# All gates leave PSUM as tanh of half their input: Silu and Sigmoid taken out of a hybrid encoder layer's later stages

## The chip, the cores and the metric

The kernel runs on one core of a Trainium2 chip. The metric is device time in microseconds (us), the median of several executions. Before the change it is 1966.65 us, over three runs from 1964.79 to 1967.43 us. The engines are called as in the profile: PE is the matrix engine (PEld is its weight load), DVE the vector engine, ACT the scalar engine that evaluates activation functions, POOL the GpSimd engine, and SP the queue from which the program issues its DMAs.

## The reference: one encoder layer with two attention branches

Two groups of 1024 tokens with 1024 channels go through the same layer. The input is normalised and modulated to `h`, and one projection `h @ w_in` gives queries, keys and values of two branches, two gate paths `za` and `zb` (512 columns each) and two merge gates `ga` and `gb` (1024 columns each):

```python
oa = gqa_attention(qa, ka, va) * jax.nn.silu(za)
ob = diff_attention(qb, kb, vb, lam)
ob = rms_norm(ob, subln_g) * (1.0 - lam_init)
ob = ob.reshape(B, S, BR_B) * jax.nn.silu(zb)
pa = jnp.einsum('bse,ed->bsd', oa, w_proj_a)
pb = jnp.einsum('bse,ed->bsd', ob, w_proj_b)
merged = jax.nn.sigmoid(ga) * pa + jax.nn.sigmoid(gb) * pb
out = jnp.einsum('bsd,de->bse', merged, w_out)
return x + gate[:, None, :] * out
```

Branch A is grouped-query attention with 8 heads; its softmax denominators are divided out late, when the gate is applied. Branch B is differential attention with 4 heads of two softmax maps each. With `silu(z) = z * sigmoid(z)` and `sigmoid(z) = (tanh(z/2) + 1) / 2`, both gate functions can be written with tanh.

## The kernel before, in words

Large products are made in two-part float32r form: each operand is split into a high and a low part, and three matmuls stand for one. The two token groups (`g` 0 and 1) run one after the other, each in these stages. The **head** makes keys, values and the first queries of branch A. **Phases 0 to 4** run attention units (score matmuls at lines 709 and 710, row maximum on DVE at line 711, exponential on ACT at line 712, a transpose on DVE at line 753, value matmuls at 768 and 785) while the input projections for later heads are made beside them. The **gated stretch** runs the last head of attention beside `gated_gen`, which multiplies attention outputs by their gates, and beside the start of the merge. Then come **merge** (`merge_gen`, line 915) and **output projection** (`out_gen`, line 944), which are almost all matmul.

The gate projections are made by `z_gen`, in twelve items per group, each of four PSUM banks of 128 x 512 (24 matmuls per bank, line 679). They are cut into small steps and woven into all stages up to the gated stretch, where they keep PE fed. Items 0 to 3 (16 banks per group) are `za` and `zb`; items 4 to 11 are `ga` and `gb`. Each bank is copied by ACT to an SBUF tile `ev` (line 685; the pool holds one such tile) and stored to DRAM by a DMA (line 688). Of the items, five banks' worth of steps lie in the head of group 0 and four in that of group 1.

In `gated_gen` the attention output `o` and the gate `z` come back by DMA (lines 867 and 868), ACT applies Silu to `z` (line 870), DVE multiplies `o` by `z` (line 875 in branch A, 881 in branch B, there with the column `subg`) and by the softmax or norm factor (line 885), and the product is split for the projection: its high part on ACT (line 886), its low part on DVE (line 887). In `merge_gen` two gate tiles at a time come back (line 905), ACT applies Sigmoid to both (line 906), and DVE multiplies the projected branch in PSUM by the gate (line 926 for branch A, 921 for branch B).

The order of instructions on each engine is set when the kernel is built: the generators are woven by tables of weights at the top of the file, attention steps have priority, and the tile framework's scheduler then places each instruction by its own model of durations. Each engine runs its list strictly in that order; SP too issues its DMAs in list order, and each waits there for its data. PSUM banks rotate: the pool `f` has three, `s` two of double width, `a` one.

## Time and profile before

| what | value |
| --- | --- |
| median of three runs | 1966.65 us (1964.79 to 1967.43) |
| the profiled execution's own time | 1970.28 us |
| its span, first to last instruction | 1968.4 us |
| busy, PE / DVE / ACT / POOL | 1900.2 / 1110.0 / 861.2 / 723.6 us |
| mean granted TensorE clock | 0.983 |

The profile is of one execution, which was 3.6 us slower than the median. An activation function outside the set that ACT holds needs an `ACT_TABLE_LOAD` before it, which the profile lists as an instruction of the line that needs it. In rows of the timeline the columns are start in us, duration in us, engine, line, operation, output `<-` inputs, shapes and count; a bracket at the end gives the idle time of the engine before it and what ended that. In rows of grouped instructions a bar separates busy time and mean duration from the idle time before them. `zd` are the gates stored in DRAM, `row` and `q` the SBUF tiles of the gated stretch, `p` the tiles of 128 x 1024 that hold exponentials and also merge gates, `st` weights as they are loaded.

### The profile page before, as it was taken

What the parts mean: (1) busy time and instruction counts of PE and PEld (TensorE: products, weight loads), DVE (VectorE), ACT (ScalarE), POOL (GpSimd) and SP (SyncE); (2) the same over time, 40 slices, a digit from 0 to 9 for tenths busy, and PEclk for the clock granted to TensorE, in tenths of its full rate; (3) what the DMA queues carried; (4) which work ended last, traced back from release to release, by engine and by line L of the source; (5) the groups of instructions that cost most, each with busy time, mean ns of one, the idle gap of its engine ahead of it and who ended that gap; (6) DMA issues with size and microseconds to landing.
All of it is one profiled execution on the core that took longest, in us unless ns stands there. A gap on an engine that the chain in (4) does not pass through costs nothing.

```text
span 1968.4 us, 29657 instructions
## 1 busy us (share of the span) xinstructions
PE 1900.2 (97%) x10466; PEld 1574.4 (80%) x10466; DVE 1110.0 (56%) x1570; ACT 861.2 (44%) x1653; POOL 723.6 (37%) x1008
## 2 busy tenths in 40 slices
PE   8899999999999998899999999999999999999999
PEld 3788778888888984778889788888888798877887
DVE  5557762444667466647464667444447735665641
ACT  4434442444445344754323445333445524567410
POOL 2463431433465251221236544124456616412110
PEclk9899999999999999999999999999999999999999
DMA  8125674546243335875641567655524423567531
GB/s 313 47 73 159 186 204 135 161 123 201 79 136 111 100 86 173 248 236 192 206 157 41 141 190 194 176 161 147 159 78 137 114 74 92 169 204 270 168 102 54
DMA packets 269011, 295.03 MB, mean 150 GB/s; under 512 B 35264, under 2 KB 217664, under 8 KB 268864
## 3 DMA queue, kind: packets, MB, share of 16 engines
q1 hardware_dynamic: 268864, 293.15, 49.9%
q8 instruction: 83, 1.36, 0.3%
q14 instruction: 64, 0.52, 0.1%
HBM read 133.59 MB, written 42.01 MB: 89 GB/s over the span
## 4 chain that ended last, share of the span: by engine, by line
PE 81%; DMA 6%; ACT 3%; POOL 3%; DVE 3%; issue 2%; SPq 2%; ACTq 0%; POOLq 0%; DVEq 0%
PE f L679 21%; PE f L496 19%; PE f L915 6%; PE a L768 6%; PE f L944 5%; PE s L709 5%; PE s L710 5%; PE s L944 4%; PE a L785 4%; PE s L915 2%; DMA row<-zd 1%; SPq L762 1%; DMA st<-in_w_in_dram 1%; PE f L547 1%; DMA q<-p 1%
## 5 line engine op out<-in xcount | busy, mean ns | idle before, releaser
L679 PE MATMUL f<-u,w 128*128 128x512 f32 x2232 | 579.3, 398 | 1.7 <-ACT w L178 1.2
L496 PE MATMUL f<-w,u 128*128 128x256 f32 x3456 | 483.6, 286 | 2.5 <-ACT ev L685 1.6
L679 PEld LDWEIGHTS f<-u,w 128*128 128x128 f32 x2232 | 411.4, 190 | 85.3 <-issue 2.7
L496 PEld LDWEIGHTS f<-w,u 128*128 128x128 f32 x3456 | 456.3, 192 | 24.1 <-issue 2.3
L711 DVE TENSOR_REDUCE m<-s 128x1 f32<-128x1024 f32 x256 | 310.2, 1219 | 240.6 <-PE s L710 238.5
L712 ACT ACTIVATE p<-s,m 128x1024 f32<-128x1024 f32 x256 | 285.1, 1114 | 241.3 <-DVE m L711 208.8
L180 POOL TENSOR_TENSOR w<-st,w 128x512 fp32r<-128x512 f32 x168 | 220.9, 1332 | 456.4 <-ACT w L178 410.9
L753 DVE STREAM_TRANSPOSE p<-p 128x1024 f32<-128x1024 f32 x192 | 237.3, 1240 | 70.3 <-ACT p L712 61.7
L514 POOL TENSOR_TENSOR rs<-ss,nhalf 128x4 f32<-128x4 f32 (+1 forms) x112 | 110.0, 982 | 329.9 <-DVE ss L513 275.2
L710 PE MATMUL s<-u,sw 128*128 128x512 f32 x512 | 206.2, 403 | 0.0
L178 ACT ACTIVATE w<-st 128x512 fp32r<-128x512 f32 x196 | 114.6, 626 | 136.0 <-DMA st<-in_w_in_dram 79.7
L915 PE MATMUL f<-u,w 128*128 128x512 f32 x552 | 134.6, 398 | 4.4 <-ACT ev L685 3.7
L785 PE MATMUL a<-q,u 128*128 128x256 f32 x512 | 130.2, 393 | 7.3 <-DMA q<-p 5.5
L915 PEld LDWEIGHTS f<-u,w 128*128 128x128 f32 x552 | 104.7, 192 | 26.8 <-ACT ev L685 3.9
L709 PE MATMUL s<-u 128*128 128x512 f32 x256 | 111.2, 434 | 12.2 <-ACT p L712 12.0
L550 DVE TENSOR_TENSOR u<-f,u 64x256 fp32r<-64x256 f32 (+1 forms) x196 | 80.4, 411 | 71.3 <-ACT u L549 66.4
L768 PE MATMUL a<-q,u 128*64 128x256 f32 x1024 | 117.7, 382 | 0.8 <-DMA q<-p 0.8
L785 PEld LDWEIGHTS a<-q,u 128*128 128x128 f32 x512 | 99.0, 198 | 23.8 <-issue 7.8
L710 PEld LDWEIGHTS s<-u,sw 128*128 128x128 f32 x512 | 98.3, 192 | 17.4 <-issue 0.8
L709 PE MATMUL s<-u,u 128*128 128x512 f32 x256 | 104.7, 410 | 4.3 <-ACT p L712 3.4
L944 PE MATMUL f<-u,w 128*128 128x512 f32 x456 | 105.6, 389 | 0.0
L508 ACT ACTIVATE row<-f 128x256 f32<-128x256 f32 (+1 forms) x112 | 41.1, 367 | 146.1 <-PE f L496 135.5
(169 smaller groups left out, 2140.9 us busy)
## 6 DMA issues: line engine op xcount, KB each, us to landing
q<-p SPq DMA_DIRECT2D x768, 128.0 KB, 2.6
st<-in_w_in_dram SPq DMA_DIRECT2D x132, 256.0 KB, 3.1
zd<-ev SPq DMA_DIRECT2D x96, 256.0 KB, 2.5
sw<-u SPq DMA_DIRECT2D x256, 64.0 KB, 2.0
p<-zd SPq DMA_DIRECT2D x64, 256.0 KB, 3.8
u<-in_w_ada_dram SPq DMA_DIRECT2D x8, 1024.0 KB, 10.4
od<-oo SPq DMA_DIRECT2D x64, 128.0 KB, 2.4
st<-in_w_in_dram SPq DMA_DIRECT2D x64, 128.0 KB, 2.7
```

Source lines behind the costliest of these rows:

```text
L180: e.tensor_tensor(out=wl, in0=st, in1=wh.bitcast(F32), op=ALU.subtract)
L496: nc.tensor.matmul(ps, lt[c][:, sl], w[:, c, wi, :], start=(k == 0), stop=(k == 23))
L679: nc.tensor.matmul(ps, w[:, c, wi, e * P : (e + 1) * P], rt[c], start=(k == 0), stop=(k == 23),)
L709: nc.tensor.matmul(s[:, sl], q, k[:, sl], start=True, stop=False)
L710: nc.tensor.matmul(s[:, sl], sw, k[:, sl], start=False, stop=True)
L711: nc.vector.tensor_reduce(out=m, in_=s, axis=AX.X, op=ALU.max, negate=True)
L712: nc.scalar.activation(pt.rearrange("p (j c a) -> p j c a", j=4, c=8), s.rearrange("p (c a j) -> p j c a", c=8, j=4), AF.Exp, bias=m, accu ...
L753: nc.vector.transpose(pt, pt)
L768: lambda k=k, m=m: nc.tensor.matmul(acc[(LO, HI)[m]], u["v"][:, k], pT[m][:, k], start=(k == 0), stop=(k == 7))
L785: nc.tensor.matmul(acc, u["v"][:, k], pT[:, k], start=(k == 0), stop=(k == 7))
L915: nc.tensor.matmul(ps, w[:, c, wi, d * P : (d + 1) * P], o[:, oi, :], start=(k == 0), stop=(k == 11))
L944: nc.tensor.matmul(ps, w[:, c, wi, e * P : (e + 1) * P], m[:, mi, :], start=(k == 0), stop=(k == 23))
```

## The change

`z_gen` now leaves PSUM by `tanh(z/2)` for every item. For `za` and `zb` a second instruction, on DVE, makes `(tanh + 1) * z` in the same tile, reading the PSUM bank once more; that is twice Silu. `gated_gen` no longer applies Silu, and `merge_gen` no longer applies Sigmoid: its multiply by the gate becomes `(tanh + 1) * projected`, one instruction as before. The halves are folded into `subg` (branch B), into the reciprocal softmax sums as they leave PSUM (branch A), and into the output gate column `gatec`.

```diff
@@ load_tables_B, gate_gen
-        nc.vector.tensor_scalar(out=subg, in0=subg, scalar1=(1.0 - LAM_INIT) * math.sqrt(2 * HD), scalar2=None, op0=ALU.mult)
+        nc.vector.tensor_scalar(out=subg, in0=subg, scalar1=0.5 * (1.0 - LAM_INIT) * math.sqrt(2 * HD), scalar2=None, op0=ALU.mult)
...
+            nc.vector.tensor_scalar(out=gatec[:, cs], in0=gatec[:, cs], scalar1=0.5, scalar2=None, op0=ALU.mult)
@@ z_gen
                 ev = mtile("ev", [P, 512], bufs=1)
-                nc.scalar.activation(ev, ps, fn)
+                nc.scalar.activation(ev, ps, AF.Tanh, scale=0.5)
+                if silu:
+                    nc.vector.scalar_tensor_tensor(out=ev, in0=ev, scalar=1.0, in1=ps, op0=ALU.add, op1=ALU.mult)
@@ gated_gen
-            nc.scalar.activation(row, ps, AF.Copy)
+            nc.scalar.activation(row, ps, AF.Copy, scale=0.5)
...
-            if i >= SILU:
-                nc.scalar.activation(z, z, AF.Silu)
@@ merge_gen
-                        nc.scalar.activation(gg, gg, AF.Sigmoid)
...
-                        nc.vector.tensor_tensor(out=g, in0=ps, in1=g, op=ALU.mult)
+                        nc.vector.scalar_tensor_tensor(out=g, in0=g, scalar=1.0, in1=ps, op0=ALU.add, op1=ALU.mult)
...
-                        nc.vector.tensor_tensor(out=md[:, d], in0=ps, in1=g, op=ALU.mult)
+                        nc.vector.scalar_tensor_tensor(
+                            out=md[:, d], in0=g, scalar=1.0, in1=ps, op0=ALU.add, op1=ALU.mult
+                        )
@@ z_item: za and zb pass silu=True, ga and gb do not
```

Line numbers shift by one or two in the changed kernel: the copy out of PSUM is line 684 there and the new DVE instruction 686, the row maximum is 712, the exponential 713, the multiply by the gate 874, the next multiply 884, the split 885 and 886. In the whole program the list of ACT has 43 table loads before and 2 after (one for the first Silu at the start, one for exponential and tanh). DVE has 34 instructions more: 32 at line 686 and two on `gatec`.

The first place is ACT in the gated stretch of group 1. Before, `row` at line 870 is a gate tile under Silu, with table loads on both sides of the exponentials of line 712:

```order
L685 ACTIVATE ev_16787<-f_16748 128x512
L886 ACTIVATE u_16735<-row_16791 128x512
L870 ACTIVATE row_16856<-row_16856 128x512
L712 ACT_TABLE_LOAD
L712 ACTIVATE p_16882,su_16883<-s_16885,m_16884 128x1024
L712 ACTIVATE p_16938,suB_135<-s_16940,m_16939 128x1024
L886 ACTIVATE u_16854<-row_16855 128x512
L870 ACT_TABLE_LOAD
L870 ACTIVATE row_16918<-row_16918 128x512
L685 ACTIVATE ev_16878<-f_16816 128x512
```

The same piece in the changed kernel:

```order
L684 ACTIVATE ev_16784<-f_16745 128x512
L885 ACTIVATE u_16733<-row_16788 128x512
L713 ACTIVATE p_16877,su_16878<-s_16880,m_16879 128x1024
L713 ACTIVATE p_16932,suB_135<-s_16934,m_16933 128x1024
L885 ACTIVATE u_16850<-row_16851 128x512
L684 ACTIVATE ev_16873<-f_16812 128x512
```

The four instructions of Silu and its loads are gone, and what is left keeps its order.

The second place is DVE in the same stretch. Before, with the first multiply by the gate at line 875, the row maximum at 711 and the weighting of the second softmax map at 752:

```order
L887 TENSOR_TENSOR u_16735<-row_16791,u_16735 128x512
L875 TENSOR_TENSOR row_16855<-row_16855,row_16856 128x512
L711 TENSOR_REDUCE m_16939<-s_16940 128x1
L737 RECIPROCAL r_16892<-su_16883 128x1
L885 TENSOR_TENSOR row_16855<-tab_16860,row_16855 128x512
L752 SCALAR_TENSOR_TENSOR p_16845<-p_16882,r_16892,p_16845 128x1024
```

and in the changed kernel:

```order
L874 TENSOR_TENSOR row_16851<-row_16851,row_16852 128x512
L800 COPY ssB_136<-f_16890 128x2
L886 TENSOR_TENSOR u_16733<-row_16788,u_16733 128x512
L712 TENSOR_REDUCE m_16933<-s_16934 128x1
L884 TENSOR_TENSOR row_16851<-tab_16855,row_16851 128x512
L738 RECIPROCAL r_16887<-su_16878 128x1
L753 SCALAR_TENSOR_TENSOR p_16841<-p_16877,r_16887,p_16841 128x1024
```

The multiply by the gate stood behind the previous split (887 before, 886 after) and now stands ahead of it, still ahead of a row maximum; its second operand now comes straight from a DMA.

The third place is DVE in the head of group 0, at the second bank of `za`. Before (line 378 splits `h`, 527 to 536 are the rotary step):

```order
L378 TENSOR_TENSOR u_549<-u_188,u_548 128x512
L527 TENSOR_TENSOR rc_612<-row_601,tab_389 128x128
L535 TENSOR_TENSOR row_601<-row_601,tab_391 128x4x16 x2
L378 TENSOR_TENSOR u_549<-u_188,u_548 128x512 x2
L536 TENSOR_TENSOR row_601<-rc_612,row_601 128x128
```

and in the changed kernel:

```order
L526 TENSOR_TENSOR rc_613<-row_602,tab_389 128x128
L534 TENSOR_TENSOR row_602<-row_602,tab_391 128x4x16 x2
L376 TENSOR_TENSOR u_550<-u_188,u_549 128x512
L686 SCALAR_TENSOR_TENSOR ev_658<-ev_658,f_577 128x512
L535 TENSOR_TENSOR row_602<-rc_613,row_602 128x128
```

The new instruction, which is the last reader of its PSUM bank, stands behind two rotary steps and a split of `h`.

More of the change, by code (lines that the diff above doesn't have):

```diff
@@ L59 @@
 LAG = 2
-SILU = 0
 CUTS = (3, 6)
@@ L665, in vb_gen, with z_gen @@
             yield 1
-    def z_gen(ht, col, dst, i0, fn=AF.Copy):
+    def z_gen(ht, col, dst, i0, silu=False):
         w = load_w(w_cols(w_in, (col, 256)))
@@ L1023, in z_item @@
         ht = st["ht"]
-        fn = AF.Silu if i < SILU else AF.Copy
         if i < 2:
-            return z_gen(ht, C_ZA + i * 256, st["zd"], i * 2, fn)
+            return z_gen(ht, C_ZA + i * 256, st["zd"], i * 2, True)
         if i < 4:
-            return z_gen(ht, C_ZB + (i - 2) * 256, st["zd"], i * 2, fn)
+            return z_gen(ht, C_ZB + (i - 2) * 256, st["zd"], i * 2, True)
         i -= 4
```

## The prediction

> **What bounds the kernel now.** I read the engines' totals first, then busy time by stretches, then the idle times of PE one by one. In the totals the columns are busy us, share of the span and count; in the stretches they are busy us and count per engine, granted clock, DMA share and GB/s.
>
> ```profile
> PE 1900.2 (97%) x10466; PEld 1574.4 (80%) x10466; DVE 1110.0 (56%) x1570; ACT 861.2 (44%) x1653; POOL 723.6 (37%) x1008
> ...
> 150.00:530.00 380.00, 379.34 (x2266) 310.72 (x2266) 201.90 (x233) 160.85 (x323) 136.23 (x194) 1.00 0.56 159
> 740.00:875.00 135.00, 121.28 (x491) 86.43 (x492) 78.77 (x108) 79.50 (x114) 29.32 (x38) 0.95 0.72 226
> 1125.00:1500.00 375.00, 374.20 (x2257) 308.95 (x2256) 203.46 (x237) 160.22 (x323) 143.20 (x208) 1.00 0.56 156
> 1725.00:1810.00 85.00, 76.48 (x329) 61.71 (x328) 53.56 (x76) 63.90 (x86) 16.90 (x17) 0.94 0.75 246
> ```
>
> PE is busy 97% of the span and the change takes no matmul away, so only PE's 68 us of idle time and its slow clock can be won. In phases 0 and 1 (150 to 530, 1125 to 1500) it idles 0.7 and 0.8 us: nothing is to be had there, and anything added there can only cost. The two gated stretches (740 to 875, 1725 to 1810) idle 13.7 and 8.5 us, and there ACT has its largest share, 59% and 75%. The single idle times, in the timeline of PE, with the one of the head that the change touches:
>
> ```profile
> 77.55 3.62 PE L496 MATMUL f<-w,u 128*128 128x256 f32 x28 [1.65 <-ACT ev L685]
> ...
> 801.30 0.50 PE L679 MATMUL f<-u,w 128*128 128x512 f32 x1 [1.21 <-ACT w L178]
> 824.27 1.01 PE L797 MATMUL f<-ones_c,at 128*128 128x1 f32 x4 [3.83 <-ACT ev L685]
> 848.08 0.65 PE L880 MATMUL f<-ident,ssB 128*128 128x128 f32 x4 [2.75 <-ACT ev L685]
> 853.96 3.06 PE L915 MATMUL f<-u,w 128*128 128x512 f32 x12 [0.67 <-DVE u L926]
> ...
> 1754.38 0.55 PE L709 MATMUL s<-u 128*128 128x512 f32 x1 [2.13 <-ACT p L712]
> 1766.42 0.50 PE L709 MATMUL s<-u 128*128 128x512 f32 x1 [2.01 <-ACT p L712]
> 1782.92 8.03 PE L915 MATMUL f<-u,w 128*128 128x512 f32 x22 [3.69 <-ACT ev L685]
> ```
>
> The last seven add up to 16.3 us. Six wait for ACT, the seventh for a DVE product whose gate comes from ACT. So ACT, at 44% over the span, bounds these places by the order of its list.
>
> **What is removed.** The instructions that go, in ACT's groups (busy us, mean ns):
>
> ```profile
> L906 ACT ACTIVATE p<-p 128x1024 f32<-128x1024 f32 x32 | 33.8, 1059 | 40.1 <-DMA p<-zd 37.1 <-DVE u L926 1.8 <-DVE q L885 1.0
> L870 ACT ACT_TABLE_LOAD x20 | 25.7, 1283 | 16.3 <-DMA row<-zd 16.1
> L712 ACT ACT_TABLE_LOAD x13 | 16.7, 1283 | 0.2
> L870 ACT ACTIVATE row<-row 128x512 f32<-128x512 f32 x24 | 15.1, 630 | 7.1 <-DMA row<-zd 6.9
> L906 ACT ACT_TABLE_LOAD x8 | 10.3, 1283 | 8.2 <-DMA p<-zd 8.1
> L870 ACT ACTIVATE q<-q 128x512 f32<-128x512 f32 x8 | 4.7, 624 | 0.0
> ```
>
> Loads 25.7 + 16.7 + 10.3 = 52.7 us, Silu 19.8, Sigmoid 33.8: 106 us of ACT, to which its waits for `zd` come (16.1 + 6.9 + 37.1 + 8.1 = 68 us), with the next exponential or PSUM copy queued behind. What that is worth is read at the seven stalls, from ACT's timeline just ahead of each:
>
> ```profile
> 800.62 0.63 ACT L178 ACTIVATE w<-st 128x512 fp32r<-128x512 f32 x1
> ...
> 818.26 1.28 ACT L712 ACT_TABLE_LOAD   x1
> 820.77 1.28 ACT L870 ACT_TABLE_LOAD   x1
> 822.07 0.63 ACT L870 ACTIVATE row<-row 128x512 f32<-128x512 f32 x1
> ...
> 845.19 1.28 ACT L906 ACT_TABLE_LOAD   x1 [3.53 <-DMA p<-zd]
> ...
> 1753.12 1.11 ACT L712 ACTIVATE p<-s,m 128x1024 f32<-128x1024 f32 x1
> 1763.21 0.63 ACT L870 ACTIVATE row<-row 128x512 f32<-128x512 f32 x1 [0.54 <-DMA row<-zd]
> 1763.86 1.28 ACT L712 ACT_TABLE_LOAD   x1
> 1765.16 1.11 ACT L712 ACTIVATE p<-s,m 128x1024 f32<-128x1024 f32 x1
> 1778.00 1.28 ACT L870 ACT_TABLE_LOAD   x1 [2.06 <-DMA row<-zd]
> ```
>
> and the row maxima that the two exponentials need, on DVE:
>
> ```profile
> 1750.44 1.22 DVE L711 TENSOR_REDUCE m<-s 128x1 f32<-128x1024 f32 x1
> 1761.99 1.21 DVE L711 TENSOR_REDUCE m<-s 128x1 f32<-128x1024 f32 x1
> ```
>
> Stall at 801: the weight split at 800.62 stood behind a Silu; its load may have landed late as well, so 0 to 1.21, I take 0.6. At 824: load, load and Silu, 1.28 + 1.28 + 0.63 = 3.19 of 3.83. At 848: ACT waited 3.53 us for a merge gate, then loaded a table and applied Sigmoid ahead of the PSUM copy; all 2.75. At 853.96: 0 to 0.67, I take 0.33. At 1754: the exponential could start when its maximum ends, 1750.44 + 1.22 = 1751.66, not 1753.12: 1.46 of 2.13. At 1766: 1761.99 + 1.21 = 1763.20 instead of 1765.16: 1.96 of 2.01. At 1782.92: Silu's wait, two loads and a Sigmoid stood ahead of the copy; all 3.69. Sum: 0.6 + 3.19 + 2.75 + 0.33 + 1.46 + 1.96 + 3.69 = **14.0 us**.
>
> Some of it returns. The multiply by the gate (line 874 after) now waits on DVE for the DMA of `zd` itself, with a row maximum in the list behind it, as the second listing of the change shows. DVE is busy 58% and 63% of these stretches. What is late next is DVE's chain from gate to split and the projection weights. Bounds: nothing of the 14 returns, or all of it; I take a quarter, the end nearest to the rows, since at 1763.21 the gate had landed and the maximum had still been made first. That leaves **10.5 us**.
>
> **The clock.** PE runs at half speed after such stalls:
>
> ```profile
> 820.00:830.00 10.00, 6.17 (x18) 4.73 (x18) 5.81 (x7) 8.89 (x13) 4.27 (x6) 0.66 0.65 202
> 1750.00:1760.00 10.00, 7.87 (x30) 6.22 (x30) 6.79 (x10) 7.37 (x11) 0.34 (x1) 0.83 0.78 238
> 1780.00:1790.00 10.00, 7.08 (x19) 5.62 (x20) 5.81 (x9) 9.89 (x13) 3.82 (x3) 0.66 0.99 343
> ```
>
> A mean of 0.66 is 6.8 us at half speed, 0.83 is 3.4 us. Less the idle time that lies in them (3.83, 2.13, 2.92 us), PE worked 3.0, 1.3 and 3.9 us at half speed and lost half of that, 4.1 us. Bounds 0 to 4.1; I take half, **2 us**, since other waits of about 2 us stay. The Trainium skill ("TensorE: Matmul & The Clock Gate", section "Part 1: The HAM clock gate") says that the clock halves after an idle window of some 3.4 us; by that rule, if every stall falls below 3.4 us, all 4.1 would come back and the sum be 2 us better. The trace agrees only in part: the slice with a stall of 2.13 us slowed too.
>
> **What is added.** The price of the new instruction is not in the trace; the nearest rows are the same operation reading PSUM at the same size (line 949) and, for the merge, the multiply that it replaces (line 926). Behind them, DVE ahead of the place in the head, and SP's longest waits for the copy:
>
> ```profile
> L949 DVE SCALAR_TENSOR_TENSOR q<-f,gatec,q 128x512 f32<-128x512 f32 x19 | 14.2, 748 | 46.1 <-PE f L944 46.1
> L926 DVE TENSOR_TENSOR u<-f,p 128x512 f32<-128x512 f32 x28 | 19.3, 688 | 30.6 <-PE f L915 29.9 <-ACT p L906 0.5
> ...
> 77.51 0.35 DVE L535 TENSOR_TENSOR row<-row,tab 128x64 f32<-128x64 f32 x2
> 77.78 1.29 DVE L378 TENSOR_TENSOR u<-u,u 128x512 fp32r<-128x512 f32 x2
> ...
> SPq L688 <- ACT ev L685: 114.5, 33, 16.7
> ```
>
> 32 new ones at 0.75 us are 24 us of DVE. Each also keeps its PSUM bank longer, and the store behind it on SP. *Head of group 0, second bank:* PE already waits there for this bank (77.55). The new instruction stands behind the two rotary steps and one split: from the row at 77.78 the split ends at about 78.45, plus 0.75 is 79.2, against a copy that ended at 77.5: **1.7 us**. *The other eight banks of the heads:* 0 to 8 x 0.75 = 6 us; PE found a bank free there, so I take **1.3**. *The 23 banks of phases 0 and 1:* 0 to 23 x 0.75 = 17 us; covered by the third bank of the pool and by DVE's idle time (380 - 201.9 = 178 us in the first of them); since PE's order is reshuffled there and has nothing to gain, I take **2**. *SP:* the 32 stores of `za` and `zb` start later by about 0.75 us plus DVE's queue, with weight loads and attention's transposes queued behind; SP already waits 114.5 us in this manner without PE idling, so 0; if that cover is gone it is another 0.75 each, inside the 17 above. *Merge:* 64 multiplies become 748 - 688 = 60 ns longer, 3.8 us of DVE beside matmuls: 0. *The halves* ride on scale operands, or are two multiplies of 8 columns: 0. *tanh for a copy* on ACT: taken as equal, 0.
>
> **Sum.** -10.5 - 2 + 1.7 + 1.3 + 2 = -7.5 us: 1970.28 becomes 1962.8 in the profiled execution, and the median 1966.65 becomes **1959**.
>
> The Trainium skill ("ScalarE: Activation LUTs", section "What ACT_TABLE_LOAD costs") puts a switch of sets at 1283 ns plus a drain of 1380 ns, about 2.66 us. By that, the stalls at 824, 1754 and 1766 would close entirely and the sum be 0.64 + 0.67 + 0.05 = 1.4 us better. The trace agrees with 1283 but shows no drain: Silu ends at 1763.84, the load starts at 1763.86 and the exponential at 1765.16.
>
> **The rivals.** *Everything comes back* (faster): the 14.0 and 4.1 us in full, and only the known 1.7 us lost: -16.4, 1950 us. For it: ACT loses 106 us of work just where PE waits for it. Against: DVE is next in line.
>
> *The stalls move to DVE* (no change): the waits for `zd`, 68 us on ACT, now stand on DVE ahead of row maxima. Then the seven stalls give back only the loads that stood in them without a wait (at 824 two, at 1754 and 1766 one each, 4 x 1.28 = 5.1 us), the clock gives nothing, and the additions cost 5: 1966.5 us. For it: the second listing. Against: before, the same DMA wait plus Silu already delayed the same multiply.
>
> *Two-step evacuation starves PE of banks* (slower): each of the 32 banks waits for an ACT copy, then for a DVE instruction queued behind a maximum or transpose of 1.2 us. At 0.75 plus half of 1.2 that is 1.35 us per bank, 43 us in all; if half reaches PE, 22 us are lost against the 12.5 won: +9, 1976 us. It decides from 12.5 / 32 = 0.4 us per bank. Against: in phases 0 and 1 PE idles 0.2% now; for it: no stretch there has slack of its own.
>
> *The change doesn't do what it says*, tanh needing a table of its own beside the exponential: then each bank would bring two loads, 96 x 2 x 1.28 = 246 us on ACT. The list with only two loads speaks against it.
>
> **How the numbers follow.** Forecast 0.40, everything back 0.18, moved to DVE 0.20, starved 0.21, own table 0.01. A measurement of this kernel tells about 0.2%, 3.9 us, from no change. The forecast (own range 1954 to 1964) lies almost wholly below 1962.7; with the second case and a little of the third that gives faster 0.60; same 0.19; slower 0.21. The range runs from just under the second case to near the fourth, 1948 to 1974.
>
> **What would show it.** Two table loads left; ACT busy near 861 - 106 = 755 us, DVE near 1110 + 24 + 4 = 1138. PE's idle time falls from 13.7 to about 6 in the first gated stretch and from 8.5 to about 3 in the second, and the slices at half clock shrink. The stall at 77.55 grows to about 3.3 us, and phases 0 and 1 together idle under 4 us. I am wrong if PE waits in phases 0 and 1 for line 686, or if PE's waits in the gated stretches only change their name to DVE.

## The result, and the profile after

The changed kernel takes **1960.64 us** (median of five runs, 1957.10 to 1963.12) against 1966.94 us for the kernel before on the same chip (five runs, 1964.79 to 1968.65): a ratio of 0.9956 with an interval of 0.9941 to 0.9972, so it is faster by 0.44%. A second measurement on another chip gave 1959.15 us and 0.9964 [0.9951, 0.9977]. The forecast was 1959 us. The profiled execution took 1963.12 us with a span of 1961.3 us and a mean granted clock of 0.984.

The engines' totals of the page of the kernel after (busy us, share of the span, count):

```profile
PE 1898.5 (97%) x10466; PEld 1575.0 (80%) x10466; DVE 1129.1 (58%) x1604; ACT 761.0 (39%) x1548; POOL 723.7 (37%) x1008
```

ACT lost 100 us and DVE gained 19. The groups of the kernel after that the prediction had to price without a row of their own (busy us, mean ns, then the idle time before them and what ended it):

```profile
L684 ACT ACTIVATE ev<-f 128x512 f32<-128x512 f32 x93 | 55.3, 595 | 110.8 <-PE f L678 85.1 <-DMA zd<-ev 12.1 <-DMA q<-p 6.8
L337 ACT ACT_TABLE_LOAD x1 | 1.3, 1283 | 0.7 <-PEq L1125 0.7
L411 ACT ACT_TABLE_LOAD x1 | 1.3, 1283 | 0.0
...
L686 DVE SCALAR_TENSOR_TENSOR ev<-ev,f 128x512 f32<-128x512 f32 x29 | 19.6, 677 | 22.6 <-ACT ev L684 22.3
L924 DVE SCALAR_TENSOR_TENSOR u<-p,f 128x512 f32<-128x512 f32 x28 | 19.0, 684 | 24.4 <-PE f L913 24.4
...
L686 DVE SCALAR_TENSOR_TENSOR ev<-ev,s 128x512 f32<-128x512 f32 x3 | 2.1, 688 | 3.0 <-ACT ev L684 3.0
...
L874 DVE TENSOR_TENSOR row<-row,row 128x512 f32<-128x512 f32 x16 | 11.2, 698 | 12.2 <-DMA row<-zd 12.2
L880 DVE SCALAR_TENSOR_TENSOR row<-row,subg,row 128x512 f32<-128x512 f32 x8 | 6.0, 751 | 19.4 <-DMA row<-zd 19.2 <-DMA q<-zd 0.2
```

The tanh takes 595 ns, as long as the copy did (594). Two table loads are left. The new instruction takes 677 to 688 ns, less than the 748 that were taken for it, and the merge multiply 684, no more than the 688 of the multiply that it replaced. The waits for `zd` now stand on DVE (lines 874 and 880), as the prediction said.

**Where the time went.** To compare two executions whose stages lie at different times, I cut both at the same points of the work: for each group the end of three quarters (192 of 256) of branch B's value matmuls, and the end of the last merge matmul. The first cut lies where the gated stretch begins. So a stretch "head and phases" runs from the group's start to the first cut, and a stretch "gated and merge" between the two; what follows is output projection alone. In the rows, the columns are the stretch, its length, then busy us and count of PE, PEld, DVE, ACT and POOL, granted clock, DMA share and GB/s. Before:

```profile
0.00:748.40 748.40, 718.60 (x4194) 593.81 (x4195) 417.00 (x606) 320.12 (x667) 308.52 (x462) 0.98 0.48 140
748.40:937.00 188.60, 176.63 (x755) 132.37 (x753) 120.89 (x170) 107.80 (x154) 38.64 (x36) 0.98 0.69 219
1024.90:1702.00 677.10, 663.02 (x4010) 566.80 (x4009) 387.99 (x555) 294.46 (x625) 308.02 (x455) 0.99 0.47 133
1702.00:1877.50 175.50, 166.99 (x739) 136.85 (x738) 114.20 (x154) 102.73 (x144) 34.23 (x32) 0.97 0.62 200
```

and after:

```profile
0.00:754.20 754.20, 721.01 (x4194) 596.75 (x4195) 425.27 (x622) 320.61 (x667) 305.40 (x462) 0.98 0.48 139
754.20:933.40 179.20, 174.12 (x754) 130.18 (x753) 123.10 (x171) 58.24 (x103) 41.11 (x36) 1.00 0.72 230
1021.40:1703.90 682.50, 665.65 (x4009) 568.26 (x4008) 396.62 (x571) 294.23 (x624) 307.30 (x455) 0.98 0.47 132
1703.90:1870.30 166.40, 162.66 (x738) 135.13 (x738) 114.46 (x156) 53.07 (x93) 35.50 (x32) 0.99 0.66 211
```

The counts of PE agree within one in each pair of rows, so the same matmuls lie between the cuts, and a difference in PE's busy time is its clock, the order of its matmuls or the way their ends are modelled, not other work. Gated and merge shrink from 364.1 to 345.6 us: **18.5 us gained**, of which 11.7 are idle time of PE (12.0 + 8.5 before, 5.1 + 3.7 after) and 6.8 are busy time (343.6 to 336.8). Head and phases grow from 1425.5 to 1436.7 us: **11.2 us lost**, 6.2 of idle time (43.9 to 50.0) and 5.0 of busy time. Part of the busy time is the clock of this one execution: by the clock's records PE had half speed for 51.2 us of these stretches before and for 58.0 after, and for 54.6 in a second profile of the changed kernel, which loses 8.6 us there. The output projections change by 0.2. Together that is -7.1 us, the difference of the two profiled executions (1970.28 to 1963.12). So the small net gain is a large gain and a large loss.

The idle times of PE of 0.7 us and more that matter, after (timeline of PE; the bracket is the idle time and what ended it):

```profile
80.83 4.28 PE L495 MATMUL f<-w,u 128*128 128x256 f32 x21 [2.64 <-ACT u L607]
...
199.07 0.70 PE L678 MATMUL f<-u,w 128*128 128x512 f32 x2 [0.74 <-DVE ev L686]
238.40 1.91 PE L769 MATMUL a<-q,u 128*64 128x256 f32 x15 [1.95 <-DMA st<-in_w_in_dram]
269.10 3.01 PE L495 MATMUL f<-w,u 128*128 128x256 f32 x23 [1.12 <-DVE ev L686]
...
635.43 0.50 PE L710 MATMUL s<-u 128*128 128x512 f32 x1 [1.64 <-ACT p L713]
...
830.89 4.42 PE L678 MATMUL f<-u,w 128*128 128x512 f32 x18 [1.01 <-ACT ev L684]
837.37 2.83 PE L786 MATMUL a<-q,u 128*128 128x256 f32 x12 [0.93 <-DMA q<-p]
...
1102.43 0.80 PE L710 MATMUL s<-u,u 128*128 128x512 f32 x1 [3.64 <-ACT p L713]
...
1779.58 2.84 PE L913 MATMUL f<-u,w 128*128 128x512 f32 x8 [3.74 <-DVE u L924]
```

Of the seven stalls in the gated stretches (16.3 us) 5.7 us are left, in three others (1.01, 0.93, 3.74). Ahead of them new ones have come: two name line 686 itself, and the rest wait for a weight load, for exponentials, and for the copy of values out of another PSUM bank (line 607). The stall of 3.74 us is the one place where a wait moved to DVE, as its timeline there shows:

```profile
1778.17 0.75 DVE L880 SCALAR_TENSOR_TENSOR row<-row,subg,row 128x512 f32<-128x512 f32 x1 [5.89 <-DMA row<-zd]
1778.84 0.68 DVE L924 SCALAR_TENSOR_TENSOR u<-p,f 128x512 f32<-128x512 f32 x1
```

DVE waited 5.89 us for a gate, and the merge multiply on which PE waited stood behind it. The three slices that ran slow before (granted clock, third column from the end: 0.66, 0.83 and 0.66) are after:

```profile
820.00:830.00 10.00, 9.67 (x44) 7.45 (x42) 7.81 (x9) 4.72 (x8) 6.86 (x6) 1.00 0.80 243
1750.00:1760.00 10.00, 10.00 (x48) 8.30 (x47) 7.79 (x12) 3.78 (x8) 0.34 (x1) 1.00 0.82 268
1780.00:1790.00 10.00, 10.00 (x43) 8.46 (x42) 4.74 (x10) 1.65 (x3) 1.27 (x1) 0.83 0.97 327
```

Of 17.0 us at half speed (6.8 + 3.4 + 6.8) 3.4 are left, behind the stall of 3.74 us.

### The profile page after: what moved, and what is told of

Its sections match the earlier page's. It is cut to its first block, busy times and chain, and to the rows that moved or that the text cites. A ratio compares the mean times of both kernels' runs of the same rounds, so it can differ in the third digit from the quotient of the medians.

```text
span 1961.3 us, 29552 instructions
## 1 busy us (share of the span) xinstructions
PE 1898.5 (97%) x10466; PEld 1575.0 (80%) x10466; DVE 1129.1 (58%) x1604; ACT 761.0 (39%) x1548; POOL 723.7 (37%) x1008
## 5 line engine op out<-in xcount | busy, mean ns | idle before, releaser
L913 PEld LDWEIGHTS f<-u,w 128*128 128x128 f32 x552 | 103.3, 188 | 25.5 <-DVE u L924 4.2
L769 PEld LDWEIGHTS a<-q,u 128*64 128x64 f32 x1024 | 73.8, 137 | 41.0 <-issue 9.9
```

Source lines behind the costliest of these rows:

```text
L769: lambda k=k, m=m: nc.tensor.matmul(acc[(LO, HI)[m]], u["v"][:, k], pT[m][:, k], start=(k == 0), stop=(k == 7))
L913: nc.tensor.matmul(ps, w[:, c, wi, d * P : (d + 1) * P], o[:, oi, :], start=(k == 0), stop=(k == 11))
```

## The experiments

Two questions were open: whether the gain comes from the table loads or from all the ACT work that is gone, and what in the new DVE product costs the loss. The table collects all kernels. Lengths and idle times of PE (us) are sums over both groups of rows cut at the same points as the eight above, each from the kernel's own profile. The profiled executions lie up to 4 us from the medians (fourth column), and the two profiles of the changed kernel differ by 2.6 and 1.3 us in length; smaller differences are not read.

| kernel | median | ratio [95%] | profiled | head and phases: length, idle | gated and merge: length, idle |
| --- | --- | --- | --- | --- | --- |
| before | 1966.94 | 1 | 1970.28 | 1425.5, 43.9 | 364.1, 20.5 |
| the change | 1960.64 | 0.9956 [0.9941, 0.9972] | 1963.12 | 1436.7, 50.0 | 345.6, 8.8 |
| the change again | 1959.15 | 0.9964 [0.9951, 0.9977] | 1959.15 | 1434.1, 51.1 | 344.3, 8.0 |
| change without the product | 1951.16 | 0.9912 [0.9898, 0.9927] | 1951.52 | 1425.4, 45.1 | 345.2, 9.2 |
| before with the product | 1977.12 | 1.0057 [1.0043, 1.0070] | 1975.06 | 1431.1, 50.8 | 363.1, 21.7 |
| before without loads | 1949.87 | 0.9912 [0.9898, 0.9927] | 1952.56 | 1424.8, 46.6 | 347.0, 11.6 |
| tanh for the merge only | 1961.82 | 0.9971 [0.9959, 0.9983] | 1961.82 | 1423.1, 45.5 | 357.9, 15.6 |
| late product | 1965.49 | 0.9993 [0.9980, 1.0006] | 1964.83 | 1422.6, 43.8 | 361.5, 18.4 |
| late, tanh ahead | 1966.37 | 0.9997 [0.9984, 1.0010] | 1967.41 | 1421.0, 44.3 | 365.8, 24.0 |
| late for branch A only | 1969.92 | 1.0017 [1.0004, 1.0029] | 1966.05 | 1426.0, 46.4 | 359.2, 18.1 |
| quarter width | 1950.43 | 0.9916 [0.9899, 0.9934] | 1954.48 | 1428.5, 46.6 | 345.3, 8.5 |
| product from SBUF only | 1946.18 | 0.9896 [0.9880, 0.9913] | 1946.18 | 1422.5, 43.3 | 342.6, 8.1 |
| two tiles, bank left after the copy | 1958.34 | 0.9964 [0.9951, 0.9977] | 1958.34 | 1427.6, 48.4 | 350.1, 12.6 |
| two tiles, bank held | 1960.96 | 0.9971 [0.9959, 0.9982] | 1958.63 | 1434.4, 55.2 | 343.5, 7.4 |

### The change without its product

```diff
@@ z_gen of the changed kernel
                 nc.scalar.activation(ev, ps, AF.Tanh, scale=0.5)
-                if silu:
-                    nc.vector.scalar_tensor_tensor(out=ev, in0=ev, scalar=1.0, in1=ps, op0=ALU.add, op1=ALU.mult)
```

> The changed kernel without its new DVE instruction in z_gen: za and zb are stored as tanh alone, so the product with z is left out of what is computed. In the heads and phases 0 and 1 the order on PE, DVE and SP is that of the kernel before. Theory 'two terms' (by the landmarks of the two traces the gated stretches give about 20 us, and the new instruction costs about 12 us in heads, phases 0 and 1 and after): 1960.6 - 12 = 1949 us (1945 to 1953), phases 0 and 1 idle on PE under 1.5 us each as before. Rival 'not the instruction' (the loss in heads and phases is drift between executions): stays at 1957 to 1962.

Measured 1951.16 us. The 32 DVE instructions cost 1960.64 - 1951.16 = 9.5 us. All of it lies in head and phases (1425.4 us against 1436.7 and, in the second profile, 1434.1); gated and merge stay as they are after the change (345.2 and 345.6). The price takes in the new order: in head and phases of group 0, PE's first 4190 matmuls, this kernel has the order of the kernel before, and the changed kernel has a matmul of other tiles at 621 of these places.

### The product alone, in the kernel before

```diff
@@ z_gen of the kernel before
                 nc.scalar.activation(ev, ps, fn)
+                if col < C_GA and not C_QB <= col < C_ZB:
+                    nc.vector.scalar_tensor_tensor(out=ev, in0=ev, scalar=1.0, in1=ps, op0=ALU.add, op1=ALU.mult)
```

> The kernel before with the new DVE instruction added behind the copy of za and zb (it makes (z + 1) * z, so the gates are not the reference's); Silu, Sigmoid and all 43 loads stay. If the price of the instruction is its own and adds to the rest: about 10 us slower than before, 1975 to 1979 us. If it only appears together with the shorter gated stretches: no change, 1964 to 1969 us.

Measured 1977.12 us, 10.9 more than the 1966.22 of the kernel before, measured beside it. So the price comes with the product and the order that the scheduler makes for it: the loads that are still there neither hide nor enlarge it by more than 1.4 us. In the profiles head and phases grow by 5.6 us, 6.9 us more idle time and 1.3 us less busy time; the profiled execution of the kernel before was 3.3 us slower than its median. In head and phases of group 0 PE has the order of the changed kernel here. The timeline of PE in this kernel repeats stalls of the changed kernel, with the same lengths or nearly so:

```profile
196.11 0.70 PE L679 MATMUL f<-u,w 128*128 128x512 f32 x2 [0.74 <-DVE ev L687]
235.02 3.76 PE L770 MATMUL a<-q,u 128*64 128x256 f32 x32 [1.53 <-DMA st<-in_w_in_dram]
265.72 3.02 PE L496 MATMUL f<-w,u 128*128 128x256 f32 x23 [1.12 <-DVE ev L687]
...
633.39 0.50 PE L711 MATMUL s<-u 128*128 128x512 f32 x1 [1.64 <-ACT p L714]
```

Line 687 is the product here. At the places of the first three neither the kernel before nor the change without the product idles for 0.5 us, and where the fourth stands these two stall for 0.55 and 0.44 us on a rotary step. So the late weight load and the late exponential come with the product and its order too, though the trace names other lines for them.

### The loads alone

```diff
@@ gated_gen and merge_gen of the kernel before
-                nc.scalar.activation(z, z, AF.Silu)
+                nc.scalar.activation(z, z, AF.Tanh, scale=0.5)
...
-                        nc.scalar.activation(gg, gg, AF.Sigmoid)
+                        nc.scalar.activation(gg, gg, AF.Tanh, scale=0.5)
```

> The kernel before with Silu and Sigmoid replaced in place by tanh (z is not multiplied in, so the gates are not those of the reference): the 41 table loads go, every other instruction, wait and the order on all engines stay. Theory 'loads': at the seven stalls the loads that stood in them come out, 0.6 + 2.57 + 1.28 + 1.28 + 1.28 + 2.57 = 9.6 us, and 2 us of clock: about 1955 us (1951 to 1958). Rival 'list order' (what held PE was ACT waiting for gates in its list and the activations, not the loads): 1961 to 1965. A result at 1947 or less would say that the loads are the whole gain of the gated stretches.

Measured 1949.87 us. Every engine keeps its order; only 41 loads go. Its groups on ACT and its rows of the gated stretches:

```profile
L906 ACT ACTIVATE p<-p 128x1024 f32<-128x1024 f32 x32 | 33.9, 1059 | 49.4 <-DMA p<-zd 37.6 <-DVE u L926 11.7
L870 ACT ACTIVATE row<-row 128x512 f32<-128x512 f32 x24 | 15.1, 629 | 33.6 <-DMA row<-zd 33.6
```

```profile
749.30:929.70 180.40, 173.50 (x755) 130.50 (x754) 121.67 (x169) 82.32 (x135) 39.98 (x36) 1.00 0.71 228
1693.20:1859.80 166.60, 161.86 (x739) 133.98 (x738) 115.93 (x155) 76.94 (x124) 35.60 (x32) 1.00 0.64 211
```

In these two rows ACT still does 49 us of gate functions and still waits 71 us for `zd` (37.6 + 33.6), and yet the gated stretches take 347.0 us, 17.1 less than before. The change without the product, in which this work and these waits are gone as well, gains 18.9 there, and its time is the same (1951.16 and 1949.87). So the gain comes from the table loads; the gate functions themselves and ACT's waits were covered, up to the 1.8 us between the two; the two profiles of the changed kernel differ by 1.3 us there. Per load that is 17.1 / 41 = 0.42 us at the end, of 1.283 us each. The expected 1951 to 1958 was too little a gain: idle time gave 8.9 us where 9.6 were counted, but PE's busy time 8.3 where 2 were.

### Tanh for the merge gates only

```diff
@@ z_gen of the changed kernel
-                nc.scalar.activation(ev, ps, AF.Tanh, scale=0.5)
-                if silu:
-                    nc.vector.scalar_tensor_tensor(out=ev, in0=ev, scalar=1.0, in1=ps, op0=ALU.add, op1=ALU.mult)
+                nc.scalar.activation(ev, ps, AF.Copy) if silu else nc.scalar.activation(ev, ps, AF.Tanh, scale=0.5)
@@ gated_gen
+            nc.scalar.activation(z, z, AF.Silu)
```

> Only ga and gb leave PSUM as tanh and the merge multiplies by (tanh + 1); za and zb are copied and Silu stays on ACT in the gated stretch, with its loads (29 loads in all, 43 before). No DVE instruction is added. Theory 'loads': of the stalls, 848 goes (2.75), 853.96 goes (0.67), 1782.92 loses one load and one Sigmoid (2.3): -5.7 and about 1 us of clock, 1960 us (1957 to 1963). Rival 'Silu alone matters': no change, 1965 to 1968.

Measured 1961.82 us, as expected. Without the product, head and phases stay where they were before (1423.1 us). The loads that remain:

```profile
L868 ACT ACT_TABLE_LOAD x14 | 18.0, 1283 | 17.2 <-DMA row<-zd 17.2
L711 ACT ACT_TABLE_LOAD x13 | 16.7, 1283 | 0.2
```

27 of 41 are still there, 14 are gone, and the gated stretches gain 6.2 us: 0.44 us per load if all of it is put down to them (the Sigmoids are gone too), nearly the price above. This half of the change alone is worth as much as the whole of it (1961.82 and 1960.64, whose intervals overlap).

### The product late, where Silu stood

A copy leaves PSUM for `za` and `zb`, and tanh and the product follow in `gated_gen`. In the first kernel they stand behind the multiply by the gate:

```diff
@@ z_gen: Copy for za and zb; gated_gen, behind the multiplies of the changed kernel
+            nc.scalar.activation(z, z, AF.Tanh, scale=0.5)
...
+            nc.vector.scalar_tensor_tensor(out=o, in0=z, scalar=1.0, in1=o, op0=ALU.add, op1=ALU.mult)
```

> The reference's result by another way: ga and gb leave PSUM as tanh; za and zb are copied as before, and the gated stretch makes tanh(z/2) on ACT after the multiply by z, then multiplies by (tanh + 1) on DVE: no load, no addition in heads and phases 0 and 1, but 32 tanh (20 us) stay on ACT and 32 DVE instructions (32 x 0.68 = 22 us) come to the gated stretches. 'Two terms': heads and phases as before, gated gain somewhat less than 20: 1953 us (1949 to 1957), faster than the change. Rival 'DVE is next in line there' (DVE was busy 58% and 63% of these stretches before and gets 11 us more in each): 1960 to 1967.

Measured 1965.49 us, no faster than before. The rival, by which DVE is next in line there, had the number. In the second kernel branch B makes tanh and product ahead of its own multiply, so that they can run before the attention output is there:

```diff
@@ gated_gen, branch B
+                th = mtile("tab", [P, 512])
+                nc.scalar.activation(th, z, AF.Tanh, scale=0.5)
+                nc.vector.scalar_tensor_tensor(out=z, in0=th, scalar=1.0, in1=z, op0=ALU.add, op1=ALU.mult)
```

> The late product of the former run, for branch B with tanh made into a tile of its own as soon as z has landed and the product before the multiply by o, so that it is off the chain from o to the split; branch A as in that run. The reference's result. Theory 'chain' (the late product lost its gain because tanh and product stood one after the other behind the multiplies): 1953 to 1958 us. Rival 'DVE is next in line' (32 more instructions in stretches where PE waits for DVE, wherever they stand): 1963 to 1967.

Measured 1966.37 us: it doesn't matter on which side of branch B's multiply the product stands, so the theory of a longer chain falls there. The rows of both kernels for the gated stretches, first the late product, then tanh ahead:

```profile
746.90:934.30 187.40, 178.93 (x755) 133.80 (x753) 134.13 (x187) 67.87 (x119) 41.01 (x36) 0.97 0.69 220
1698.00:1872.10 174.10, 164.19 (x739) 135.59 (x738) 126.83 (x172) 62.88 (x109) 35.34 (x32) 0.98 0.61 202
```

```profile
744.30:931.80 187.50, 176.64 (x755) 131.73 (x754) 134.08 (x187) 67.52 (x119) 40.79 (x36) 0.99 0.69 221
1696.40:1874.70 178.30, 165.21 (x739) 134.89 (x738) 127.80 (x172) 62.45 (x109) 35.44 (x32) 0.99 0.61 197
```

DVE has 261 us of work there instead of 238 without loads (121.67 + 115.93), and the two stretches take 361.5 and 365.8 us instead of 347.0. So 23 to 24 us more on DVE cost 14.5 to 18.8 us at the end. In the second kernel PE's timeline names DVE for it:

```profile
1785.47 0.65 PE L880 MATMUL f<-ident,ssB 128*128 128x128 f32 x4 [3.35 <-DVE u L929]
...
1816.37 3.00 PE L918 MATMUL f<-u,w 128*128 128x512 f32 x12 [1.27 <-DVE row L887]
```

Head and phases meanwhile cost nothing (1422.6 and 1421.0 us). The third kernel has the product late for branch A only and in `z_gen` for branch B:

```diff
@@ z_item: za leaves PSUM by Copy, zb by tanh and product; gated_gen as in the first kernel where e < 4
+            if e < 4:
+                nc.scalar.activation(z, z, AF.Tanh, scale=0.5)
```

> The product of za late, in the gated stretch, where the last attention units keep PE fed; the product of zb in z_gen as in the change, so 16 new DVE instructions in phases 0 and 1 and none in the heads. The reference's result. If prices add (about 10 us for 32 in z_gen, about 14 us for 32 late): 5 + 7 above 1951, so 1960 to 1963 us. If the head's share is the larger part of the price in z_gen and branch A's late product is free: 1953 to 1957, faster than the change.

Measured 1969.92 us, worse than either number and the one kernel of the series with all gates as tanh that is slower than before. Its profiled execution was 3.9 us faster than its median, so the rows of the table don't show all of the loss; what they show is that a half late is enough to lose most of the gain in the gated stretches (359.2 us). Why the median is worse than that of the whole product late stays open.

### What in the product costs

The product does two things in `z_gen`: it takes DVE's time, and it keeps the PSUM bank until DVE has read it. One kernel shortens both, the other reads the tanh twice instead of the bank, so that DVE works as long but the bank is free after ACT:

```diff
@@ z_gen, quarter width
-                    nc.vector.scalar_tensor_tensor(out=ev, in0=ev, scalar=1.0, in1=ps, op0=ALU.add, op1=ALU.mult)
+                    eh, ph = ev[:, :128], ps[:, :128]
+                    nc.vector.scalar_tensor_tensor(out=eh, in0=eh, scalar=1.0, in1=ph, op0=ALU.add, op1=ALU.mult)
@@ z_gen, from SBUF only
-                    nc.vector.scalar_tensor_tensor(out=ev, in0=ev, scalar=1.0, in1=ps, op0=ALU.add, op1=ALU.mult)
+                    nc.vector.scalar_tensor_tensor(out=ev, in0=ev, scalar=1.0, in1=ev, op0=ALU.add, op1=ALU.mult)
```

> The changed kernel with the new DVE instruction on 128 of 512 columns only (the product with z is left out for the rest): still one DVE instruction per bank that reads PSUM after ACT, but short, about 0.3 us (rows of 128 x 128 multiplies: 0.29 us) against 0.68. The price of the whole instruction was 1960.6 - 1951.2 = about 10 us. Theory 'DVE time' (its length counts): 10 x 0.3 / 0.68 = 4, so 1955 us. Rival 'second reader' (that the bank waits for DVE's list, and the order that follows, whatever the length): 1958 to 1961.

> The changed kernel with the new DVE instruction reading ev twice instead of ev and PSUM, so (t + 1) * t instead of (t + 1) * z: same length on DVE, same store behind it, but the PSUM bank is free after ACT as in the kernel before. Theory 'bank' (the price comes from PSUM banks held until DVE gets there): about 1951 us (1949 to 1954). Rival 'DVE time and queues' (the price is DVE's time, the later store on SP and the new order): 1958 to 1961.

Measured 1950.43 and 1946.18 us; by the whole time the price is gone in both. For the first that is less than either theory said (1955, and 1958 to 1961). The product of the first, at a quarter of the width, and that of the second, from SBUF, in their groups:

```profile
L687 DVE SCALAR_TENSOR_TENSOR ev<-ev,f 128x128 f32<-128x128 f32 x29 | 8.0, 277 | 32.9 <-ACT ev L684 32.8
```

```profile
L686 DVE SCALAR_TENSOR_TENSOR ev<-ev 128x512 f32<-128x512 f32 x32 | 25.5, 797 | 18.9 <-ACT ev L684 18.6
```

The second is the telling one: DVE works 25.5 us there, more than the 21.7 of the change (19.6 + 2.1), and PE idles 43.3 us in head and phases, as little as before (43.9). So DVE's time alone does not bring the price. Nor does the later store: SP waits 54.3 us for the product there, and 56.2 in the change. It came out below the 1951 that the bank theory expected, and below the change without the product as well; the scheduler had put group 0 in another order (303 of the 4190 places), and the first scores came 4.6 us earlier than in that kernel, which the bank can't explain.

To try the same with all work done, the last pair has a second tile. ACT copies the bank to `ev`, then makes tanh by halves into `th`, from `ev` (the bank is left after the copy) or from the bank (it is held for two more ACT instructions); the product of `th` and `ev` follows on DVE, in both from SBUF:

```diff
@@ z_gen, bank left after the copy (held: ps[:, hs] in the tanh)
+                    nc.scalar.activation(ev, ps, AF.Copy)
+                    for h2 in range(2):
+                        hs = slice(h2 * 256, h2 * 256 + 256)
+                        th = mtile("at", [P, 256], bufs=1)
+                        nc.scalar.activation(th, ev[:, hs], AF.Tanh, scale=0.5)
+                        nc.vector.scalar_tensor_tensor(
+                            out=ev[:, hs], in0=th, scalar=1.0, in1=ev[:, hs], op0=ALU.add, op1=ALU.mult
+                        )
```

> The reference's result, with the bank freed early: za and zb are copied out of PSUM as in the kernel before, then ACT makes tanh of each half from SBUF into a tile of 128 x 256, and DVE the product from SBUF. 64 half tanh on ACT (row of a 128 x 256 ACT operation: about 0.38 us, 24 us in all in heads and phases) and 64 half products on DVE come in place of 32 whole products. Theory 'bank': the price goes, 1948 to 1954 us, faster than the change. Rival 'DVE time, ACT time and order': 1958 to 1966 us.

> Twin of the run before with the same instructions, but tanh reads each half from PSUM, so that the bank is held until the second tanh, which waits for DVE's first half product. Theory 'bank': slower than its twin by most of the price, 1958 to 1963 us. Rival: the same as its twin within 3 us.

Measured 1958.34 and 1960.96 us, and 1959.15 for the change beside them. By the whole time the bank theory fell: it had expected 1948 to 1954 for the first, and the rival had the number (1958 to 1966). The second fits both, within 1958 to 1963 and within 3 us of its twin. By stretches the pair says more. In head and phases the one that leaves the bank is 6.8 us shorter (1427.6 against 1434.4) and PE idles 6.8 us less (48.4 against 55.2), as the bank theory has it. In the gated and merge stretches it loses 6.6 us again (350.1 against 343.5). The largest stall there, in the timelines of PE, the bank left and then held:

```profile
832.01 4.51 PE L794 MATMUL a<-q,u 128*128 128x256 f32 x12 [4.39 <-DMA q<-p]
```

```profile
835.31 3.69 PE L794 MATMUL a<-q,u 128*128 128x256 f32 x16 [1.05 <-DMA q<-p]
```

PE waits 3.3 us longer for an attention transpose there. What made it late was not tried; the two kernels differ in the scheduler's order as well as in the bank.

One stretch of the traces tells the kernels apart better than the sums: phases 0 and 1 of group 0, cut from the group's first matmul of line 710 (as numbered before) to its 129th of 256. It holds the same 2062 or 2063 matmuls in every kernel, and in the change 12 of the 32 products. With the quarter width, with the bank left, and with the bank held:

```profile
144.70:496.90 352.20, 347.62 (x2063) 283.60 (x2062) 182.79 (x212) 147.32 (x290) 118.43 (x157) 1.00 0.58 164
```

```profile
144.00:492.40 348.40, 347.12 (x2062) 284.98 (x2061) 191.13 (x224) 154.64 (x314) 118.82 (x156) 1.00 0.59 166
```

```profile
144.90:499.90 355.00, 348.82 (x2062) 285.30 (x2061) 192.08 (x225) 154.17 (x315) 121.70 (x160) 1.00 0.58 163
```

PE idles 4.6, 1.3 and 6.2 us. In all eight kernels in which ACT alone empties these banks it is 0.3 to 1.5 us (before 0.7, product from SBUF 1.4), in the three with the whole product from the bank 3.5 to 4.2, and 2.5 where only branch B's are. So here the price of the quarter width is not gone, though its stalls name attention transposes (1.49 and 1.84 us) and not line 687; it is won back elsewhere. The bank is kept for less time in it: DVE is done with it 0.69 us after ACT on the mean of the 32 banks, against 1.23 us in the change. But this does not single out the bank, for two reasons. In the same stretch of group 1 the two sorts of kernels do not differ (3.8 to 7.6 us and 4.6 to 7.4). And the kernels with more idle time are also those whose order differs most: of PE's first 4190 places, 613 to 648 have another matmul than before in the change, the kernel before with the product, the quarter width and the bank held, 220 to 303 in the split by branch, the product from SBUF and the bank left, and none in the others. No run changes the bank without the order.

### The change again

No edit: the changed kernel was measured once more beside the last kernels of the series.

> The changed kernel once more, beside its variants on one chip: 1957 to 1963 us, ratio near 0.9956.

Measured 1959.15 us, 0.9964 [0.9951, 0.9977]. The result holds on a second chip.

No kernel that does all the work is clearly faster than the change: the best, with two tiles and the bank left early, equals it within the interval. The 1950 us of the kernels without loads and without the price of the product were reached only by kernels that leave computation out.

## Why the prediction was right, and where its steps were not

The time was right, 1959 against 1960.64 and 1959.15, within the likeliest case's own range. That it came within 2 us is luck, since two of its terms were wrong by about as much in opposite directions:

| term | forecast | measured |
| --- | --- | --- |
| PE's idle time, gated and merge | -10.5 | -11.7 |
| clock, gated and merge | -2 | -6.8 (PE's busy time) |
| head and phases | +5 (1.7 + 1.3 + 2) | +11.2 and +8.6 in the two profiles of the change; 9.5 and 10.9 by the medians of the two experiments |
| sum (with 0.2 in the output projections) | -7.5 | -7.1 in the profiles, -6.3 by the medians |

**The seven stalls, and the quarter that returns.** Right. Of the 16.3 us of stalls 5.7 are left, 10.6 are gone, and what returned is one stall of 3.74 us on DVE, behind a wait for `zd`, close to the quarter of 14 us (3.5) that was set aside. At 824, 848 and 1782.92 the prediction had also priced the gate functions and ACT's waits for gates; the kernel without loads keeps both and gains 17.1 of the 18.5 us, so the loads were the step that counted.

**The clock.** Mis-sized: 2 taken, bounds 0 to 4.1, against 6.8 us that PE's busy time lost. The step that failed is "less the idle time that lies in them": it took all idle time of the 10 us slices off the half-speed time, but most of each stall lies ahead of it. The half-speed time before, cut at the clock's own changes:

```profile
822.85:829.68 6.83, 5.41 (x15) 4.44 (x16) 5.37 (x7) 5.75 (x9) 3.72 (x5) 0.50 0.70 213
1754.69:1758.10 3.41, 3.41 (x10) 2.74 (x9) 1.89 (x2) 1.72 (x4) 0.28 (x1) 0.50 0.87 271
1781.99:1788.82 6.83, 5.90 (x14) 4.65 (x15) 2.77 (x5) 6.78 (x11) 3.82 (x3) 0.50 0.99 342
```

PE works in 14.7 of these 17.1 us, not in 8.2, so they cost it 7.4 us, and that was the upper bound. After the change 3.4 us are left, with PE at work throughout, which cost 1.7. So the clock gave back 5.7 of the 6.8 us; for the rest the records show no cause. Taking half of the bound because "other waits of about 2 us stay" was wrong too: only the stall of 3.74 us left a slow slice. The Trainium skill ("TensorE: Matmul & The Clock Gate", section "Part 1: The HAM clock gate") has the clock halve after an idle window of some 3.4 us. The trace agrees only in part: in the gated stretches after the change there is slow time behind 3.74 us and none behind 1.01, but before, a stall of 2.13 us had brought 3.4 us of it, and in the head after the change the stall of 2.64 us at 80.83 is followed by as much.

**What is added.** Mis-sized, 5 against 9.5 to 11.2. *The second bank of the head* was said to lose 1.7; its stall grew from 1.65 to 2.64 us, 1.0, and the copy of line 607, out of another bank, is now named as last. PE goes on at 80.83 us, before DVE is done with the bank of `za` (81.35). PE's idle time up to the group's first scores did not clearly grow in sum (19.2 us before, 17.8 and 20.3 in the two profiles of the change). *The 23 banks of phases 0 and 1* were given 2 us within 0 to 17, since the third bank of the pool and DVE's idle time (178 us) would cover them. That step failed: neither covered the product. DVE's time alone is not what costs: with DVE as busy and the bank free early, PE idles as little as before (43.3 and 43.9 us). The idle times fit a price for keeping the bank: in head and phases they are 43.3 to 46.6 us in the eight kernels with no bank kept, or kept only for a quarter-width read, 48.4 with the two tiles and the bank left early, 50.0 to 51.1 in the three with the whole product from the bank, and 55.2 where two more ACT instructions hold it. (The kernel split by branch, which keeps half of the banks, has 46.4.) The Trainium skill ("PSUM — Partial Sum Buffer", section "Summary: rules for kernel authors") says to evacuate promptly. No run here tests that by itself: 9.5 us is the price of 32 banks kept for one DVE instruction more, together with the new order. The trace names line 686 at only 1.9 us of idle time (0.74 + 1.12); the rest comes in other names, as a weight load (1.95) and an exponential (1.64 at 635). The 3.64 us for an exponential at 1102 are not the product's: the change without it idles 1.64 and 2.05 us at that place. As the scheduler's order changes with each of these edits, its share is not separated. That the bank is what costs is supported by phases 0 and 1 of group 0, not shown.

**The sign said to be wrong came.** "I am wrong if PE waits in phases 0 and 1 for line 686": it does. Phases 0 and 1 of the two groups after, by stretches of the same work and nearly the same length as the prediction's:

```profile
150.00:532.00 382.00, 377.94 (x2259) 310.69 (x2258) 208.97 (x241) 161.02 (x320) 133.85 (x190) 1.00 0.56 157
1122.00:1500.00 378.00, 376.37 (x2264) 310.48 (x2264) 209.54 (x249) 161.66 (x325) 143.56 (x207) 1.00 0.56 156
```

PE idles 4.1 us in the first and 1.6 in the second, not under 4 together.

**Prices.** The new instruction was taken at 748 ns and took 677 to 688; the merge multiply was given 60 ns more and got none; DVE rose by 19 us and not by 28. Tanh for a copy at 0 was right, ACT came to 761 us for a forecast of 755.

**The rivals.** *Everything comes back* had the gated stretches right (14.0 + 4.1 = 18.1 said, 18.5 measured) and fell by the price of the product, of which it counted only 1.7. *The stalls move to DVE* fell for the change: one of the stalls moved. It is no idle fear, though: as soon as the product itself stood there, the time was 1965.5 to 1966.4 us and PE waited for DVE. *Starved of banks* was right in direction and too high in price: 9.5 to 10.9 us for 32 banks are 0.30 to 0.34 us each, against 0.68 assumed; it would have decided from 18.5 / 32 = 0.58. *A table of its own for tanh* fell with two loads left.

So the likeliest case came true in its sum. Its mechanism is shown: loads ahead of PE's operands on ACT's list in the gated stretches (the kernel without loads), against a price of the product elsewhere (the product alone in the kernel before). What stays open is how the price comes about, by the bank or by the order, and why the pair with two tiles gives back in one stretch what it wins in the other.

## What to carry to other kernels

A table load that costs ACT little over the span can still stand ahead of the one operand that PE waits for; look for it in the timeline ahead of PE's stalls, and ask of a change of function first which table it needs, not how much work it saves (41 loads gave 17 us, 54 us of gate functions at most 1.8). When work moves into the evacuation of PSUM in stages where PE has no slack, do not count on the engine's idle time or on spare banks to cover it: the bank is kept longer and the scheduler's order changes, and here the two together cost about 10 us. And measure the gain and the price apart, by doing one part alone: here a price of about 10 us and a gain of about 17 hid behind a net of 6.3 us.

## What the runs showed of the hardware that was not expected

- The multiply-add of 128 x 512 from PSUM took 677 to 688 ns with the constant 1.0 as its scalar, and the same operation with a column as scalar (line 949) 748 ns. Operand order differs too, so no run separates the two. The plain multiply from PSUM took 688, so adding the constant was free.
- The same operation with both inputs in SBUF took as long as with one in PSUM in 26 of 32 instructions (649 to 693 ns, against 648 to 690); the other six took 985 to 1725 ns and bring the mean to 797. What lengthened them was not tried.
- All 43 loads of the kernel before take 1283 ns, and those that wait for no data start 17 to 19 ns after the activation ahead of them (one 66 ns), but 1.28 us on ACT were worth 0.42 to 0.44 us at the end, in two kernels with different numbers of them (41 and 14 removed).
- The half-speed time that a stall brings lies mostly behind the stall: PE was at work in 14.7 of 17.1 us of it, and lost half of that.
